# Trace of a matrix product: the order of the five-row and the twelve-row loads

## The chip, the cores and the metric

The kernel runs on one core of a Trainium2 chip. The time is device microseconds of one execution; three runs of the kernel before gave 709.28 us (median; 708.98 to 710.05).

## The reference

For eight pairs of 2176 x 2176 matrices in float32, the kernel returns the trace of each product:

```python
prod = np.matmul(a, b)                      # a, b: (8, 2176, 2176)
traces = np.diagonal(prod, axis1=1, axis2=2).sum(axis=-1)
```

The product itself is not needed: trace(A B) is the sum over all i, k of A[i, k] B[k, i], so the sum of the elementwise product of A transposed with B. Each element of a and b is read once, 303 MB in all.

## The kernel before, in words

A matrix of 2176 rows is 17 row tiles of 128 rows (`NT`). They are split into two groups of six and one of five (`SIX`, `FIVE`, `TWICE` = 12). In a group of m row tiles, partition p holds the m consecutive rows p*m to p*m + m - 1, so that each partition is filled by one long run. All loads of the loop are issued by GpSimd and cast float32 to bf16 on the way (`fetch`).

There are four large buffers in bf16. `a_six` and `b_six` hold the twelve rows of a and of b. `five` holds the five rows: first those of a, then those of b of the same batch. `at` holds the whole transposed a of one batch.

Per batch:

- TensorE transposes a in 26 tiles (`EACH`): 18 for the twelve rows, 8 for the five (`HEAD` is the count of the tiles of the group that comes first). A tile is six or five transposes of pairs of bf16 columns read as float32 (line 224), or up to fifteen of single columns (line 227). It goes into one of three PSUM slots (`slots`). TensorE waits for the load of a group on the semaphore `moved`, which SyncE counts up when a load of a has landed (lines 172 and 173), and for a free slot; it counts finished tiles in `made`.
- ScalarE evicts three of four tiles to `at` (line 269), VectorE every fourth (line 295). The first eviction of a batch waits until the products of the batch before are through, because these read `at`.
- When all 26 tiles are evicted, VectorE multiplies `at` with b and reduces (line 284): once for the twelve rows, once for the five, each as soon as its load has landed. `product` counts these, two a batch.

What sets the order of the work is written out by hand. GpSimd's queue issues, in each batch, a's twelve rows, a's five, b's twelve, b's five; each load waits on the semaphore that says that its buffer's old content is used up (`made` for a, `product` for b). Loads on one queue run one after the other. In batch 0, the first row of each partition comes by a load of SyncE in float32, lands in `b_six`, and is cast to its place by ScalarE and VectorE (lines 262 and 281).

In the last batch (`LAST`), b comes in nine pieces (`pieces`), so that little work is left behind the last bytes. `shares` says for each piece which columns VectorE multiplies; the rest goes to TensorE as 128 x 128 matmuls into `trace_ps` (line 253), whose diagonal VectorE takes at the end. The third number of a share is a count of filler matmuls, whose result is not used (line 255). A last row of small matmuls (line 333) sums over the partitions; VectorE copies the result (line 338) and SyncE stores it.

Of the kernel before, what the change touches and what calls it, by code (L numbers as in the profile page):

```python
# [21 lines left out]
def kernel(  # L22
# [6 lines left out]
    nc = tc.nc  # L29
    P = 128  # L30
    BATCH, N, N2 = a.shape
    assert N == N2 and N % P == 0
    NT = N // P
    SIX, FIVE = 6, 5
    TWICE = 2 * SIX
# [7 lines left out]
    HALF = 8 * P  # L43
# [6 lines left out]
    a_six = big.tile([P, TWICE, N], bf16, tag="a_six")  # L50
    b_six = big.tile([P, TWICE, N], bf16, tag="b_six")
    five = big.tile([P, FIVE, N], bf16, tag="five")
# [14 lines left out]
    def tiles_of(rows, start, m):  # L67

        words = rows.bitcast(f32)
        dst = at[:, :, start:start + P * m].rearrange("q v (p r) -> q v p r", r=m)  # L70
        pairs, singles = [], []
        for first, bm in groups:
            v = first // P
            if bm % 2 == 0:
                for t in range(bm // 2):
                    pairs.append((v + 2 * t, first // 2 + t, bm // 2))
            else:
                singles += [(v + r, first + r, bm) for r in range(bm)]
        for v, c0, step in pairs:
            yield (  # L80
                [(f32, r, words[:, r, c0:c0 + step * (P - 1) + 1:step]) for r in range(m)],
                dst[:, v:v + 2, :, :],
                lambda ps: ps[:, 0:m, :].bitcast(bf16).rearrange("q r (p s) -> q s p r", s=2),
            )
        each = 16 // m
        for at0 in range(0, len(singles), each):
            some = singles[at0:at0 + each]
            yield (
                [
                    (bf16, n * m + r, rows[:, r, c0:c0 + step * (P - 1) + 1:step])  # L90
                    for n, (_, c0, step) in enumerate(some) for r in range(m)
                ],
                dst[:, some[0][0]:some[0][0] + len(some), :, :],
                lambda ps, k=len(some): ps.bitcast(bf16).rearrange("q a b -> q (a b)")[
                    :, 0:k * m * P
                ].rearrange("q (n r p) -> q n p r", r=m, p=P),
            )

    six_tiles = [
        t for g in range(2)  # L100
        for t in tiles_of(a_six[:, g * SIX:(g + 1) * SIX, :], g * SIX * P, SIX)
    ]
    five_tiles = list(tiles_of(five, TWICE * P, FIVE))
    tiles = six_tiles + five_tiles
    EACH, HEAD = len(tiles), len(six_tiles)
    on_vector = [n for n in range(EACH) if n % 4 == 3]
    on_scalar = [n for n in range(EACH) if n % 4 != 3]

    def flat(t):
        return t.rearrange("p r k -> p (r k)")  # L110

    def six(src):
        return src[0:TWICE * P, :].rearrange("(g p r) k -> p g (r k)", g=2, r=SIX)

    def rows_of(src, start, m, r0, r1):
        return src[start:start + P * m, :].rearrange("(p r) k -> p (r k)", r=m)[:, r0 * N:r1 * N]

    by_twos = "p (g r) k -> p g (r k)"
# [7 lines left out]
    class Piece:  # L126
# [8 lines left out]
            self.src = src[:, r0 * N + lo:(r1 - 1) * N + hi]  # L135

    pieces = [
        Piece(0, 6), Piece(6, 10), Piece(10, 12), Piece(12, 14), Piece(14, 15), Piece(15, 16),
        Piece(16, 17, 6 * P, N), Piece(16, 17, 2 * P, 6 * P), Piece(16, 17, 0, 2 * P),
    ]  # L140


    shares = [
        (0, N, 0), (0, N, 0), (0, 0, 7), (0, 0, 6), (0, N, 0), (HALF, N, 2),
        (6 * P, 11 * P, 0), (0, 0, 0), (0, 0, 0),
    ]

    with tc.tile_critical(no_gpsimd_drain=True):  # L148
        def counted(name):
            return Counted(nc, name)  # L150

        first_row, first_five = counted("first_row"), counted("first_five")
        d_a6, d_a5, d_b6, d_b5 = (counted(f"load_{x}") for x in ("a6", "a5", "b6", "b5"))
        d_late = [counted(f"late{n}") for n in range(len(pieces))]
        zeros, ready, cast = counted("zeros"), counted("ready"), counted("cast")
        moved, made = nc.alloc_semaphore("moved"), nc.alloc_semaphore("made")
        free = [nc.alloc_semaphore(f"free{k}") for k in range(SLOTS)]
        scalar_done, vector_done = counted("scalar_done"), counted("vector_done")
        product, early, added = counted("product"), counted("early"), counted("added")
# [3 lines left out]

        sp = nc.sync
        words = flat(b_six[:, 0:2, :].bitcast(f32))
        first_row.by(sp.dma_start(out=words, in_=rows_of(a[0], 0, SIX, 0, 1)), 16)
        for n in range(BATCH):
            if n == 0:
                sp.wait_ge(cast.sem, 2)
                sp.wait_ge(first_five.sem, 16)  # L170
            for load in (d_a6, d_a5):
                sp.wait_ge(load.sem, 16 * (n + 1))
                sp.sem_inc(moved)


        gp = nc.gpsimd

        def fetch(count, dst, src):
            count.by(gp.dma_start(out=dst, in_=src), 16)  # L179

        for n in range(BATCH):
            if n == 0:
                fetch(first_five, flat(a_six[:, 1:SIX, :]), rows_of(a[0], 0, SIX, 1, SIX))
                fetch(d_a6, flat(a_six[:, SIX:, :]), rows_of(a[0], SIX * P, SIX, 0, SIX))
                gp.wait_ge(zeros.sem, 2)
                for t in (identity32, identity16):
                    ready.by(gp.affine_select(
                        out=t, in_=t, compare_op=mybir.AluOpType.not_equal, fill=1.0, base=0,
                        pattern=[[-1, P]], channel_multiplier=1,
                    ))  # L190
            else:
                gp.wait_ge(made, EACH * (n - 1) + HEAD)
                fetch(d_a6, a_six.rearrange(by_twos, g=2), six(a[n]))
                gp.wait_ge(product.sem, 2 * n)
            fetch(d_a5, flat(five), rows_of(a[n], TWICE * P, FIVE, 0, FIVE))
            if n == 0:
                gp.wait_ge(cast.sem, 2)
            else:
                gp.wait_ge(product.sem, 2 * n - 1)
            if n < LAST:  # L200
                fetch(d_b6, b_six.rearrange(by_twos, g=2), six(b[n]))
                gp.wait_ge(made, EACH * (n + 1))
                fetch(d_b5, flat(five), rows_of(b[n], TWICE * P, FIVE, 0, FIVE))
                continue
            for k, piece in enumerate(pieces):
                if piece.v0 == TWICE:
                    gp.wait_ge(made, EACH * (n + 1))
                fetch(d_late[k], piece.dst, piece.src)
        gp.drain()


# [35 lines left out]
        for w in work:  # L247
            k, x, y = w
# [10 lines left out]
        middle = N // 2  # L259
        act = nc.scalar  # L260
        act.wait_ge(first_row.sem, 16)
        cast.by(act.copy(out=a_six[:, 0, :middle], in_=words[:, :middle]))  # L262
        for n in range(BATCH):
            for t in on_scalar:
                _, dst, view = tiles[t]
# [10 lines left out]
        dve = nc.vector  # L276
# [1 line left out]
        for t in (identity32, identity16):  # L278
            zeros.by(dve.memset(t, 0.0))
        dve.wait_ge(first_row.sem, 16)  # L280
        cast.by(dve.tensor_copy(out=a_six[:, 0, middle:], in_=words[:, middle:]))  # L281

        def multiply_reduce(x, y, acc, out=None):
            return dve.tensor_tensor_reduce(  # L284
# [4 lines left out]
        for n in range(BATCH):  # L289
            for t in on_vector:  # L290
                _, dst, view = tiles[t]
                if t == on_vector[0] and n:
                    dve.wait_ge(product.sem, 2 * n)
                dve.wait_ge(made, EACH * n + t + 1)
                ins = dve.tensor_copy(out=dst, in_=view(slots[t % SLOTS]))  # L295
                if t != on_vector[-1]:
                    ins.then_inc(free[t % SLOTS], 1)
                else:
                    vector_done.by(ins)
            dve.wait_ge(vector_done.sem, n + 1).then_inc(free[on_vector[-1] % SLOTS], 1)  # L300
            dve.wait_ge(scalar_done.sem, n + 1).then_inc(free[on_scalar[-1] % SLOTS], 1)
            if n == LAST:
                continue
            for k, (load, t, v0) in enumerate(((d_b6, b_six, 0), (d_b5, five, TWICE))):
                dve.wait_ge(load.sem, 16 * (n + 1))
                product.by(multiply_reduce(
                    flat(at[:, v0:v0 + t.shape[1], :]), flat(t), sums[:, 2 * n + k:2 * n + k + 1],
                ))
        dve.wait_ge(early.sem, 1)
        dve.reduce_sum(  # L310
            out=result[:1, 0:LAST],
            in_=total[:, 0:2 * LAST].rearrange("o (b n) -> o b n", n=2),
# [3 lines left out]
        for k, (piece, (lo, hi, _)) in enumerate(zip(pieces, shares)):  # L316
            if hi > lo:
                dve.wait_ge(d_late[k].sem, 16)
                t, base = (b_six, 0) if piece.v0 < TWICE else (five, TWICE)
# [11 lines left out]
        for c in range(cols):  # L331
# [9 lines left out]
            out=out.rearrange("(a b) -> a b", a=1), in_=result[:1, :],  # L341
# [34 lines left out]
```

## Time and profile before

| | |
|---|---|
| median of the runs | 709.28 us |
| the profiled execution: span from its first to its last instruction (the page gives no other time of its own) | 706.8 us |
| share of the span in which engines are busy | PE 26%, DVE 54%, ACT 29%, POOL 4% |
| HBM read | 303.04 MB, 429 GB/s over the span |
| mean granted TensorE clock | 0.671 |

PE is TensorE's matmul, PEld its weight load, DVE VectorE, ACT ScalarE, POOL GpSimd, SP SyncE. A row of a time line is: start in us, length in us, engine, line, operation, out<-in, shapes, number of instructions merged into it, and in brackets the idle time just before it with what ended it. The length of a DMA instruction in such a row is the time that its issue took, not the transfer. A row of a group ends with: busy us, mean ns of one, and idle us before them. A row of a table of windows has the window, its length, the busy time of PE, PEld, DVE, ACT and POOL with their counts, the granted clock, the DMA share and the GB/s written.

### The profile page before, as it was taken

The page shows a single profiled execution, that of the slowest core. Times are in us where ns is not written, and L with a number is a line of the kernel's source. Part 1 is how long each engine was busy: PE and PEld are TensorE (multiplying, and loading weights), DVE is VectorE, ACT ScalarE, POOL GpSimd, SP SyncE. Part 2 cuts the span into 40 slices and gives each one's busy share as a digit, 9 for nine tenths or more (in the row PEclk, how much of TensorE's full clock was granted, in tenths as well). Part 3 has the DMA queues.
Part 4 walks back from the last instruction along what each step waited for, and adds up shares of the span by engine and source line. Part 5 has one row for each costly group of instructions (what it writes and reads, how often), then busy time and mean ns, then how long its engine had stood idle before and what let it go on. Part 6 is the DMA issues. An engine that isn't in the chain of part 4 may idle for free. (4 is left out here: it accounts for less than half of the span.)

```text
span 706.8 us, 3878 instructions
## 1 busy us (share of the span) xinstructions
PE 183.1 (26%) x1611; PEld 164.7 (23%) x1613; DVE 380.7 (54%) x94; ACT 203.8 (29%) x162; POOL 24.9 (4%) x46
## 2 busy tenths in 40 slices
PE   0083000830008200182002710027100370003706
PEld 0073000720007200172002710027100270003704
DVE  0031596315963169531794407944089440894487
ACT  1085000950009400094001930019200292002910
POOL 1000000000000000000000000000000000001010
PEclk9998555975559755597555965559655596555967
DMA  9999999999999999999999999999999999999997
GB/s 221 221 220 212 213 229 204 215 225 213 216 217 219 214 220 217 210 217 223 215 216 216 219 219 218 214 216 219 216 218 213 217 220 217 214 217 215 219 209 156
DMA packets 7702, 152.13 MB, mean 215 GB/s; under 512 B 658, under 2 KB 914, under 8 KB 1298
## 3 DMA queue, kind: packets, MB, share of 16 engines
q0 software_dynamic: 7552, 150.96, 99.7%
q1 hardware_dynamic: 146, 1.11, 0.5%
q8 instruction: 2, 0.03, 0.0%
q14 instruction: 2, 0.02, 0.0%
HBM read 303.04 MB, written 0.00 MB: 429 GB/s over the span
## 5 line engine op out<-in xcount | busy, mean ns | idle before, releaser
L269 ACT COPY at<-aT 128x1536 bf16<-128x1536 bf16 (+3 forms) x160 | 201.4, 1367 | 465.7 <-PE aT L224 465.2
L284 DVE CUSTOM_DVE_ANT_0 at<-at,b_six 128x26112 bf16<-128x26112 bf16 (+2 forms) x9 | 214.4, 23831 | 130.1 <-DMA b_six<-in_b_dram 130.0
L224 PE MATMUL aT<-identity,a_six 128*128 128x128 f32 x576 | 92.0, 324 | 482.5 <-PEq L221 482.5
L224 PEld LDWEIGHTS aT<-identity,a_six 128*128 128x128 f32 x576 | 85.7, 206 | 488.0 <-issue 487.9
L295 DVE COPY at<-aT 128x1536 bf16<-128x1536 bf16 (+1 forms) x48 | 80.1, 1669 | 183.3 <-PE aT L224 152.4
L284 DVE CUSTOM_DVE_ANT_0 at<-at,five 128x10880 bf16<-128x10880 bf16 (+3 forms) x10 | 85.0, 8501 | 1.0 <-DMA five<-in_b_dram 1.0
L227 PE MATMUL aT<-identity,a_six 128*128 128x128 bf16 x480 | 33.5, 219 | 11.6 <-PEq L221 11.4
L224 PE MATMUL aT<-identity,five 128*128 128x128 f32 x240 | 34.6, 289 | 4.4 <-PEq L221 4.4
L227 PEld LDWEIGHTS aT<-identity,a_six 128*128 128x128 bf16 x480 | 29.3, 118 | 15.6 <-issue 15.6
L224 PEld LDWEIGHTS aT<-identity,five 128*128 128x128 f32 x240 | 30.4, 198 | 7.4 <-issue 7.0
L179 POOL DMA_DIRECT2D five<-in_a_dram x8 | 4.4, 556 | 388.7 <-DVE sums L284 388.7
L179 POOL DMA_DIRECT2D five<-in_b_dram x13 | 7.1, 558 | 257.0 <-PE aT L227 257.0
L227 PE MATMUL aT<-identity,five 128*128 128x128 bf16 x200 | 13.9, 219 | 2.8 <-PEq L221 1.8
L227 PEld LDWEIGHTS aT<-identity,five 128*128 128x128 bf16 x200 | 11.9, 118 | 5.1 <-issue 5.1
L253 PE MATMUL trace_ps<-b_six,at 128*128 128x128 bf16 x34 | 3.8, 313 | 18.0 <-DMA b_six<-in_b_dram 18.0
L253 PEld LDWEIGHTS trace_ps<-b_six,at 128*128 128x128 bf16 x34 | 3.5, 149 | 18.1 <-issue 18.1
L179 POOL DMA_DIRECT2D b_six<-in_b_dram x10 | 6.6, 662 | 3.8 <-ACT a_six L262 3.8
L179 POOL DMA_DIRECT2D a_six<-in_a_dram x9 | 6.2, 688 | 1.0 <-SPq L148 1.0
L255 PE MATMUL aT<-at 128*128 128x512 bf16 x13 | 4.2, 462 | 0.3 <-issue 0.2
L253 PE MATMUL trace_ps<-five,at 128*128 128x128 bf16 x54 | 3.8, 220 | 1.6 <-DMA five<-in_b_dram 1.5
L253 PEld LDWEIGHTS trace_ps<-five,at 128*128 128x128 bf16 x54 | 3.1, 98 | 3.1 <-DMA five<-in_b_dram 2.7
L281 DVE CAST a_six<-b_six 128x1088 bf16<-128x1088 f32 x1 | 0.7, 726 | 4.8 <-DMA b_six<-in_a_dram 4.8
(19 smaller groups left out, 8.8 us busy)
## 6 DMA issues: line engine op xcount, KB each, us to landing
b_six<-in_b_dram POOLq DMA_DIRECT2D x7, 6528.0 KB, 47.6
a_six<-in_a_dram POOLq DMA_DIRECT2D x7, 6528.0 KB, 61.0
five<-in_a_dram POOLq DMA_DIRECT2D x8, 2720.0 KB, 17.4
five<-in_b_dram POOLq DMA_DIRECT2D x7, 2720.0 KB, 30.7
a_six<-in_a_dram POOLq DMA_DIRECT2D x1, 3264.0 KB, 32.2
b_six<-in_b_dram POOLq DMA_DIRECT2D x1, 3264.0 KB, 32.3
a_six<-in_a_dram POOLq DMA_DIRECT2D x1, 2720.0 KB, 17.5
b_six<-in_b_dram POOLq DMA_DIRECT2D x1, 2176.0 KB, 42.0
```

The source lines that it names most:

```text
L179: count.by(gp.dma_start(out=dst, in_=src), 16)
L224: last = pe.transpose(ps[:, place, :], src, identity32)
L227: last = pe.transpose(ps16[:, place * P:(place + 1) * P], src, identity16)
L253: ins = pe.matmul(trace_ps, x, y, start=w is real[0], stop=w is real[-1])
L255: pe.matmul(slots[0][:, 0:4, :], x, y, start=True, stop=True)
L269: ins = act.copy(out=dst, in_=view(slots[t % SLOTS]))
L281: cast.by(dve.tensor_copy(out=a_six[:, 0, middle:], in_=words[:, middle:]))
L284: return dve.tensor_tensor_reduce(out=x if out is None else out, in0=x, in1=y, scale=1.0, scalar=0.0, op0=MUL, op1=ADD, accum_out=acc,)
L295: ins = dve.tensor_copy(out=dst, in_=view(slots[t % SLOTS]))
```

## The change

The order of the groups is turned round: in each matrix the five-row group is loaded, transposed and multiplied ahead of the twelve rows. GpSimd now issues a's five rows, a's twelve, b's five, b's twelve. With it go these:

- The tiles of the five rows come first (`tiles`, `HEAD` = 8), and VectorE multiplies the five rows first.
- a's five rows wait for the five-row product of the batch before (`five` is free), a's twelve for all tiles of the batch before, b's five for the eight tiles of a's five, b's twelve for the twelve-row product of the batch before.
- In batch 0, SyncE's first row belongs to the five-row group. The twelve rows of a come in one load; before, they came as two loads of six (the first without its first row).
- In the last batch the pieces of b are: the five rows; the first six; two rows; three single rows; the last of the twelve rows in three parts. VectorE has the five, the six and parts of the last two rows; TensorE has the rest, with 21 filler matmuls (before: 15).
- GpSimd makes twenty increments of a semaphore that nothing reads, behind its last load and ahead of its drain.

```diff
-    tiles = six_tiles + five_tiles
-    EACH, HEAD = len(tiles), len(six_tiles)
+    tiles = five_tiles + six_tiles
+    EACH, HEAD = len(tiles), len(five_tiles)
...
     pieces = [
-        Piece(0, 6), Piece(6, 10), Piece(10, 12), Piece(12, 14), Piece(14, 15), Piece(15, 16),
-        Piece(16, 17, 6 * P, N), Piece(16, 17, 2 * P, 6 * P), Piece(16, 17, 0, 2 * P),
+        Piece(TWICE, NT), Piece(0, 6), Piece(6, 8), Piece(8, 9), Piece(9, 10), Piece(10, 11),
+        Piece(11, 12, 6 * P, N), Piece(11, 12, 2 * P, 6 * P), Piece(11, 12, 0, 2 * P),
     ]
...
     shares = [
-        (0, N, 0), (0, N, 0), (0, 0, 7), (0, 0, 6), (0, N, 0), (HALF, N, 2),
+        (0, N, 0), (0, N, 0), (0, 0, 7), (0, 0, 6), (0, 0, 6), (HALF, N, 2),
         (6 * P, 11 * P, 0), (0, 0, 0), (0, 0, 0),
     ]
...
-        first_row.by(sp.dma_start(out=words, in_=rows_of(a[0], 0, SIX, 0, 1)), 16)
+        first_row.by(sp.dma_start(out=words, in_=rows_of(a[0], TWICE * P, FIVE, 0, 1)), 16)
...
-                sp.wait_ge(first_five.sem, 16)
-            for load in (d_a6, d_a5):
+            for load in (d_a5, d_a6):
...
             if n == 0:
-                fetch(first_five, flat(a_six[:, 1:SIX, :]), rows_of(a[0], 0, SIX, 1, SIX))
-                fetch(d_a6, flat(a_six[:, SIX:, :]), rows_of(a[0], SIX * P, SIX, 0, SIX))
+                fetch(d_a5, flat(five[:, 1:, :]), rows_of(a[0], TWICE * P, FIVE, 1, FIVE))
+                fetch(d_a6, a_six.rearrange(by_twos, g=2), six(a[0]))
...
             else:
-                gp.wait_ge(made, EACH * (n - 1) + HEAD)
+                gp.wait_ge(product.sem, 2 * n - 1)
+                fetch(d_a5, flat(five), rows_of(a[n], TWICE * P, FIVE, 0, FIVE))
+                gp.wait_ge(made, EACH * n)
                 fetch(d_a6, a_six.rearrange(by_twos, g=2), six(a[n]))
-                gp.wait_ge(product.sem, 2 * n)
-            fetch(d_a5, flat(five), rows_of(a[n], TWICE * P, FIVE, 0, FIVE))
-            if n == 0:
-                gp.wait_ge(cast.sem, 2)
-            else:
-                gp.wait_ge(product.sem, 2 * n - 1)
+            gp.wait_ge(made, EACH * n + HEAD)
             if n < LAST:
+                fetch(d_b5, flat(five), rows_of(b[n], TWICE * P, FIVE, 0, FIVE))
+                if n == 0:
+                    gp.wait_ge(cast.sem, 2)
+                else:
+                    gp.wait_ge(product.sem, 2 * n)
                 fetch(d_b6, b_six.rearrange(by_twos, g=2), six(b[n]))
-                gp.wait_ge(made, EACH * (n + 1))
-                fetch(d_b5, flat(five), rows_of(b[n], TWICE * P, FIVE, 0, FIVE))
                 continue
             for k, piece in enumerate(pieces):
-                if piece.v0 == TWICE:
-                    gp.wait_ge(made, EACH * (n + 1))
+                if k == 1:
+                    gp.wait_ge(product.sem, 2 * n)
                 fetch(d_late[k], piece.dst, piece.src)
+        for _ in range(20):
+            gp.sem_inc(unread)
         gp.drain()
...
-        cast.by(act.copy(out=a_six[:, 0, :middle], in_=words[:, :middle]))
+        cast.by(act.copy(out=five[:, 0, :middle], in_=words[:, :middle]))
...
-        cast.by(dve.tensor_copy(out=a_six[:, 0, middle:], in_=words[:, middle:]))
+        cast.by(dve.tensor_copy(out=five[:, 0, middle:], in_=words[:, middle:]))
...
-            for k, (load, t, v0) in enumerate(((d_b6, b_six, 0), (d_b5, five, TWICE))):
+            for k, (load, t, v0) in enumerate(((d_b5, five, TWICE), (d_b6, b_six, 0))):
```

More of the change, by code (lines that the diff above doesn't have):

```diff
@@ L150, in counted @@
             return Counted(nc, name)
-        first_row, first_five = counted("first_row"), counted("first_five")
+        first_row, unread = counted("first_row"), nc.alloc_semaphore("unread")
         d_a6, d_a5, d_b6, d_b5 = (counted(f"load_{x}") for x in ("a6", "a5", "b6", "b5"))
```

## The prediction

> **What bounds the kernel now.** I read the page's slices first (is there one resource that never rests?), then the chain that ended last, then the time lines of GpSimd, ScalarE, VectorE and TensorE in the last batch. The slices and the note under the queues:
>
> ```profile
> DMA  9999999999999999999999999999999999999997
> HBM read 303.04 MB, written 0.00 MB: 429 GB/s over the span
> ```
>
> The transfers are busy from the first slice to the last but one, and no engine is. The chain (start, length, what):
>
> ```profile
> 674.65 28.38 DMA five<-in_b_dram
> ...
> 703.07 0.61 PE trace_ps L253 x6
> ...
> 703.71 0.29 DVE diagonal L284
> ...
> 704.29 0.15 DVE result L338
> ```
>
> So before the change the end is: last bytes of b at 703.03, six small matmuls, the diagonal on VectorE at 703.71, the result. Whatever the change does, it must show either as a hole in the stream of transfers or as an engine that reaches 703.71 late.
>
> How fast the stream is, I take from TensorE's first transpose of a batch, which waits for the twelve rows of a (batches 1 and 7):
>
> ```profile
> 123.10 4.34 PE L224 MATMUL aT<-identity,a_six 128*128 128x128 f32 x24 [62.38 <-PEq L221]
> ...
> 646.83 6.80 PE L224 MATMUL aT<-identity,a_six 128*128 128x128 f32 x36 [62.13 <-PEq L221]
> ```
>
> Six batches lie between: 523.73 / 6 = 87.29 us a batch of 34 row tiles, 2.567 us a row tile (1.09 MB in bf16). Twelve rows take 30.8 us, five 12.8 us.
>
> **Can the stream run dry in the new order?** The loads wait for buffers, so what counts is how long before its predecessor has landed a load is issued. GpSimd's issues in batch 7 and the six-row product of the batch before:
>
> ```profile
> 602.85 27.36 DVE L284 CUSTOM_DVE_ANT_0 at<-at,b_six 128x26112 bf16<-128x26112 bf16 x1 [18.72 <-DMA b_six<-in_b_dram]
> 630.14 0.08 DVE L284 DVE_READ_ACCUMULATOR2_ANT sums<- 128x1 f32 x1
> 630.14 11.48 DVE L284 CUSTOM_DVE_ANT_0 at<-at,five 128x10880 bf16<-128x10880 bf16 x1
> 641.55 0.08 DVE L284 DVE_READ_ACCUMULATOR2_ANT sums<- 128x1 f32 x1
> ...
> 641.93 0.56 POOL L179 DMA_DIRECT2D five<-in_a_dram  x1 [55.66 <-DVE sums L284]
> 642.48 1.60 POOL L179 DMA_DIRECT2D b_six<-in_b_dram  x3
> 672.57 3.18 POOL L179 DMA_DIRECT2D five<-in_b_dram  x6 [28.49 <-PE aT L227]
> ```
>
> Before, the tightest issue is a's five rows: at 641.93, 4.9 us ahead of 646.83, when the twelve rows were in. In the new order there are two issues to look at.
>
> b's five rows wait until the eight tiles of a's five rows are transposed, and those evictions wait for the twelve-row product of the batch before. That product starts five rows later than now: 602.85 + 5 x 2.567 = 615.69, ends 27.29 later at 642.98. ScalarE then has six of the eight tiles:
>
> ```profile
> L269 ACT COPY at<-aT 128x1280 bf16<-128x1280 bf16 x40 | 47.4, 1273 | 0.0
> L269 ACT COPY at<-aT 128x1920 bf16<-128x1920 bf16 x8 | 14.1, 1759 | 0.5
> ```
>
> 5 x 1.27 + 1.76 = 8.1 us, so at the latest at 651.1 all eight are transposed. The twelve rows of a are in at 646.83 + 12.84 = 659.67: a lead of 8.6 us. a's five rows of the next batch wait for b's five-row product: twelve rows of a in, 20.0 us of evictions (below), 0.41, 11.41 of product = 31.8 us; b's twelve rows are in 17 x 2.567 = 43.6 us after a's: a lead of 11.8. Both are longer than the 4.9 us that suffices now, so I cost the stream at nothing in all seven batches and at the start, where 17 rows are queued at once. The POOL waits that change places (the product ahead of a's loads, the count of tiles ahead of b's) hold up only those loads, and these leads are their price. At the start one load fewer is issued (a's twelve rows whole): I take 0, between -0.7, its issue, and +0.5, the small hole quoted under the rivals.
>
> Against this stands a rule: the Trainium skill, page "DMA: Bandwidth & Descriptors", section "Anatomy of one DMA", gives each GpSimd load a fixed 2.0 us beside bytes / 436 GB/s. Taken as time of the stream, an estimate from that page would make the missing load worth 2 us and the result about 710.8. But four loads of 2 x 18.9 MB read would then need 87 + 8 = 95 us a batch by it, and the trace has 87.29: the fixed part lies under the neighbours here.
>
> **The last batch, where the cost is.** The work after the last load is what moves. VectorE may multiply only when all 26 tiles of the last a are evicted. Now the twelve rows come first and ScalarE starts on them while the five are under way:
>
> ```profile
> 648.44 4.12 ACT L269 COPY at<-aT 128x1536 bf16<-128x1536 bf16 x3 [61.67 <-PE aT L224]
> 652.77 4.83 ACT L269 COPY at<-aT 128x1536 bf16<-128x1536 bf16 x4 [0.21 <-PE aT L224]
> 658.02 16.32 ACT L269 COPY at<-aT 128x1536 bf16<-128x1536 bf16 x13 [0.42 <-PE aT L224]
> ...
> 666.70 3.57 ACT L269 COPY at<-aT 128x1280 bf16<-128x1280 bf16 x3
> ```
>
> The last row (a view of a narrow window) is the first copy of a five-row tile: so the eighteen twelve-row tiles are evicted some 0.1 after 666.70, 20.0 us after the first transpose at 646.83. After the change these same eighteen tiles are all left to do when the last of a lands: eighteen tiles in the same pattern (positions 3, 7, 11 and 15 on VectorE), while the eight others are done by about 652. Evicted: 659.67 + 20.0 = 679.67, instead of 658.02 + 16.32 = 674.34. That is 5.3 us later, and the product follows there:
>
> ```profile
> 674.48 0.16 DVE L310 TENSOR_REDUCE result<-total 1x7 f32<-1x14 f32 x1 [2.78 <-ACT at L269]
> 674.75 13.76 DVE L284 CUSTOM_DVE_ANT_0 at<-at,b_six 128x13056 bf16<-128x13056 bf16 x1
> 688.44 0.08 DVE L284 DVE_READ_ACCUMULATOR2_ANT late<- 128x1 f32 x1
> ...
> 698.05 2.42 DVE L284 CUSTOM_DVE_ANT_0 at<-at,five 128x2176 bf16<-128x2176 bf16 x1 [0.39 <-DMA five<-in_b_dram]
> ...
> 700.66 1.36 DVE L284 CUSTOM_DVE_ANT_0 at<-at,five 128x1152 bf16<-128x1152 bf16 x1 [0.18 <-DMA five<-in_b_dram]
> 701.95 0.08 DVE L284 DVE_READ_ACCUMULATOR2_ANT late<- 128x1 f32 x1
> 702.42 0.82 DVE L284 CUSTOM_DVE_ANT_0 at<-at,five 128x640 bf16<-128x640 bf16 x1 [0.39 <-DMA five<-in_b_dram]
> 703.17 0.08 DVE L284 DVE_READ_ACCUMULATOR2_ANT late<- 128x1 f32 x1
> ```
>
> The first product started 0.41 after the last eviction, so now at 680.08. VectorE's share keeps its size (five, six, then 9 and 5 blocks of 128; before six, four, one, 9 and 5): 11.41 (630.14 to 641.55) + 13.69 (674.75 to 688.44) + 1.29 + 0.75 = 27.14 us from start to start, without any wait, since b's five rows are in at 672.5, the next six at 687.9, and the small pieces before VectorE gets to them. It is through at 707.22, and the diagonal starts there rather than at 703.71: **+3.5 us**. Before, the same work had slack: its waits for pieces (0.18 and twice 0.39) show VectorE ahead of the transfers.
>
> TensorE's share is also later. It starts on rows 6 and 7 one row later than on rows 10 and 11 before, and has six filler matmuls more:
>
> ```profile
> 690.36 3.79 PE L253 MATMUL trace_ps<-b_six,at 128*128 128x128 bf16 x34 [17.97 <-DMA b_six<-in_b_dram]
> 694.37 2.36 PE L255 MATMUL aT<-at 128*128 128x512 bf16 x6 [0.22 <-issue]
> 696.56 2.06 PE L253 MATMUL trace_ps<-five,at 128*128 128x128 bf16 x34
> 698.46 1.46 PE L255 MATMUL aT<-at 128*128 128x512 bf16 x6
> 700.68 0.62 PE L253 MATMUL trace_ps<-five,at 128*128 128x128 bf16 x8 [0.77 <-DMA five<-in_b_dram]
> ```
>
> 692.93 + 6.20 (34 and 7 fillers) + 2 x (0.95 + 1.46) + 0.68 + 0.8 (2 fillers) + 0.8 (12 matmuls) = 706.2. It no longer waits for pieces and would put the end 2.5 us later by itself, but it lies beside VectorE's 707.2.
>
> The twenty increments stand behind GpSimd's last load, which is issued by about 656 (nine pieces of 0.56 after 651.1). Even at a load's 0.56 each they would be over at 668, under the products; nothing waits for the count, so neither gain nor cost: 0. Without that cover, at the very end, they would be up to 11 us. The cast of the first row goes to another buffer at the same length: 0. What follows the diagonal is as before, one small matmul fewer.
>
> Sum: span 706.8 + 3.5 = 710.3. The median of the runs, 709.28, is 2.5 above the profiled span (launch and store around it), and I add the same: **712.8 us**, 0.5% slower. Against 0.2% of noise, 1.4 us, that can be told.
>
> **Terms that are not exact.** The landing at 659.67 could be 659.4, counted back 17 rows from 703.03: -0.3. Evictions of a whole batch took 28.0 us from the first transpose in batch 0 (34.78 to 62.79, the two rows below) and 27.5 in batch 7 (646.83 to 674.34): +0.5.
>
> ```profile
> 34.78 7.10 PE L224 MATMUL aT<-identity,a_six 128*128 128x128 f32 x36 [34.78 <-PEq L221]
> ...
> 46.47 16.32 ACT L269 COPY at<-aT 128x1536 bf16<-128x1536 bf16 x13 [0.42 <-PE aT L224]
> ```
> The landing of seventeen rows rests on the batches' rate; a hole as below in the first or a later batch adds up to 0.5 each, and three or four of them make +2. A VectorE path shorter than I think stops at TensorE's 706.2, +2.5. So 711.2 to 715.0.
>
> **The rivals.**
>
> TensorE ends last: if evictions end 1 us or more sooner than 679.67, the diagonal waits for its matmuls at 706.2, and the time is 711.8. Against it is only the sum above; 13 in 100.
>
> The stream runs dry: the 8.6 us lead of b's five rows is not enough, each batch has a hole. With 1 us in each of seven the last rows land 7 us later and the time is about 719.8. Against it: 4.9 us suffices now. 6 in 100.
>
> On the other side: the present 4.9 us is too short, and each batch now loses time which the longer leads give back. Three microseconds around that landing, in batch 1 and in batch 7, and the long stretch between:
>
> ```profile
> 121.00:124.00 3.00, 0.90 (x5) 0.93 (x6) 0.00 (x0) 0.00 (x0) 0.00 (x0) 0.50 0.82 167
> 644.60:647.60 3.00, 0.77 (x4) 0.80 (x5) 0.00 (x0) 0.00 (x0) 0.00 (x0) 0.50 0.99 210
> ...
> 124.00:646.00 522.00, 126.66 (x1119) 115.27 (x1118) 292.75 (x60) 150.99 (x120) 16.07 (x26) 0.64 1.01 217
> ```
>
> In batch 1 the DMA share (the last but one number) is 0.82, 0.5 us lost; seven such would be 3.8 us, and the time 709.0, no change. From 0.3 us in each batch on (2.1 in all) the result is within the noise. Against it: 0.99 in batch 7 and 1.01 over all. 5 in 100 for no change, 2 for an outright gain.
>
> **How the numbers follow.** VectorE late, 712.8: 74 in 100. With TensorE's case, 87 end slower; with the dry stream 93. Unchanged 5 and faster 2 are the regained holes. The range 711.2 to 715.0 covers the first two cases.
>
> **What would show it.** Right: the DMA rows unbroken; a's twelve rows of the last batch landing near 659.7; the last eviction near 679.7; VectorE without a wait for DMA from there to the diagonal near 707.2; the chain that ended last made of VectorE and before it ScalarE instead of DMA. Wrong: the diagonal's idle time put down to TensorE, or VectorE waiting for pieces of b (the shift was smaller), or a long wait of SyncE for a's rows in each batch (the stream ran dry).

## The result, and the profile after

| | before | after |
|---|---|---|
| median of the runs (8 each) | 709.24 us | 711.72 us (711.13 to 712.06) |
| ratio, 95% interval | | 1.0031 (1.0021 to 1.0041) |
| span of the profiled execution | 706.8 us | 709.8 us (that execution: 711.61 us) |

The change costs 2.5 us, 0.3%. The page of the changed kernel, its DMA slices and the shares of the chain that ended last:

```profile
DMA  9999999999999999999999999999999999999995
...
DVE 4%; ACT 1%; PE 0%; issue 0%; DVEq 0%
```

The transfers fill every slice but the last, as before, but the chain no longer ends in a transfer. It is now made of VectorE and, before it, ScalarE. The same chain in order of time (start, length, what):

```profile
670.50 8.87 ACT at L270 x7
...
679.50 0.16 DVE result L311
679.66 11.41 DVE at L285
...
691.08 13.67 DVE at L285
...
704.76 1.27 DVE at L285
...
706.03 0.74 DVE at L285
...
707.27 0.15 DVE result L339
```

These are ScalarE's last evictions, then the five rows, the first six rows and the two parts of rows, all on VectorE without a pause. Nothing in it waits for b. The time line of the last batch shows what each of these follows:

```profile
649.22 0.56 POOL L178 DMA_DIRECT2D five<-in_b_dram  x1 [44.26 <-PE aT L228]
649.78 4.25 POOL L178 DMA_DIRECT2D b_six<-in_b_dram  x8
659.30 6.74 PE L225 MATMUL aT<-identity,a_six 128*128 128x128 f32 x36 [10.38 <-PEq L222]
660.86 4.12 ACT L270 COPY at<-aT 128x1536 bf16<-128x1536 bf16 x3 [10.28 <-PE aT L225]
...
670.50 8.86 ACT L270 COPY at<-aT 128x1536 bf16<-128x1536 bf16 x7 [0.40 <-PE aT L225]
...
679.59 11.48 DVE L285 CUSTOM_DVE_ANT_0 at<-at,five 128x10880 bf16<-128x10880 bf16 x1
...
704.13 0.83 PE L254 MATMUL trace_ps<-b_six,at 128*128 128x128 bf16 x12
...
706.70 0.28 DVE L285 CUSTOM_DVE_ANT_0 diagonal<-identity,trace_ps 128x128 bf16<-128x128 f32 x1
```

a's twelve rows are in at 659.30, 12.5 us later than before (646.83). ScalarE evicts the eighteen tiles until 670.50 + 8.86 = 679.36. VectorE starts at 679.59 (674.75 before), and the diagonal comes at 706.70 (703.71 before), 1.7 us after TensorE's last matmul of b. So the profiled spans differ by 3.0 us and the medians by 2.5. The difference has two parts. The execution that was profiled before stood 0.5 us under the usual span of its kernel (706.8 against a median of 707.3 to 707.4 in the runs beside the variants), and this led to a second finding (below). And the time outside the span, launch and store, is not the same in both: 1.9 to 2.2 us in those runs of the kernel before, 1.7 to 1.8 in the eight of the changed kernel.

### The profile page after: what moved, and what is told of

It reads as the page before. It is cut to its first block, busy times and chain, and to the rows that moved or that the text cites. A ratio compares the mean times of both kernels' runs of the same rounds, so it can differ in the third digit from the quotient of the medians.

```text
span 709.8 us, 3904 instructions
## 1 busy us (share of the span) xinstructions
PE 207.4 (29%) x1617; PEld 187.4 (26%) x1617; DVE 380.9 (54%) x92; ACT 205.1 (29%) x162; POOL 24.8 (3%) x45
## 3 DMA queue, kind: packets, MB, share of 16 engines
q1 hardware_dynamic: 146, 1.11, 0.4%
HBM read 303.04 MB, written 0.00 MB: 427 GB/s over the span
## 5 line engine op out<-in xcount | busy, mean ns | idle before, releaser
L285 DVE CUSTOM_DVE_ANT_0 at<-at,b_six 128x26112 bf16<-128x26112 bf16 (+3 forms) x10 | 207.3, 20743 | 82.1 <-DMA b_six<-in_b_dram 82.1
L225 PE MATMUL aT<-identity,five 128*128 128x128 f32 x240 | 55.0, 419 | 367.9 <-PEq L222 367.9
L225 PEld LDWEIGHTS aT<-identity,five 128*128 128x128 f32 x240 | 47.3, 221 | 373.8 <-issue 373.8
L285 DVE CUSTOM_DVE_ANT_0 at<-at,five 128x10880 bf16<-128x10880 bf16 x8 | 91.9, 11491 | 14.3 <-ACT at L270 14.3
L228 PE MATMUL aT<-identity,five 128*128 128x128 bf16 x200 | 16.9, 258 | 0.0
L228 PEld LDWEIGHTS aT<-identity,five 128*128 128x128 bf16 x200 | 16.6, 132 | 0.4
L178 POOL DMA_DIRECT2D five<-in_b_dram x8 | 4.5, 563 | 334.5 <-PE aT L228 334.5
L254 PE MATMUL trace_ps<-b_six,at 128*128 128x128 bf16 x88 | 7.5, 254 | 14.4 <-DMA b_six<-in_b_dram 14.4
L254 PEld LDWEIGHTS trace_ps<-b_six,at 128*128 128x128 bf16 x88 | 6.9, 116 | 15.5 <-issue 14.7
L178 POOL DMA_DIRECT2D b_six<-in_b_dram x15 | 9.2, 636 | 0.0
```

The costliest lines, as they stand in the source:

```text
L225: last = pe.transpose(ps[:, place, :], src, identity32)
L228: last = pe.transpose(ps16[:, place * P:(place + 1) * P], src, identity16)
L254: ins = pe.matmul(trace_ps, x, y, start=w is real[0], stop=w is real[-1])
L285: return dve.tensor_tensor_reduce(out=x if out is None else out, in0=x, in1=y, scale=1.0, scalar=0.0, op0=MUL, op1=ADD, accum_out=acc,)
```

## The experiments

Each variant was run beside the kernel before on the same chip (whose medians there were 709.30 to 709.37 us). What is given is the median of the runs, then the ratio to the kernel before with its 95% interval.

**The increments.** Edit:

```diff
-        for _ in range(20):
-            gp.sem_inc(unread)
```

> The changed kernel without the twenty increments. Theory (VectorE's late start in the last batch is the whole cost): 711.7 us as with them, since GpSimd's last load is issued at 649.8 + 4.25 = 654.0, more than 50 us before the end. Rival (the increments delay the drain or the end): the time falls by what they cost, up to the whole 2.5 us, to 709.2.

Measured: 711.73 us, 1.0031 (1.0019 to 1.0044), the same as with them, so they cost nothing that can be measured. But the time outside the span is 1.95 to 2.18 us, and with them it was 1.72 to 1.81; the total is the same because the spans of these runs are a little shorter. So the increments may even save some 0.3 us outside the span. This is not shown: in the variants below that relieve both engines, which have the increments too, it is up to 2.7 us.

**Is it TensorE's longer list?** Edit, in the shares:

```diff
-        (0, N, 0), (0, N, 0), (0, 0, 7), (0, 0, 6), (0, 0, 6), (HALF, N, 2),
+        (0, N, 0), (0, N, 0), (0, 0, 7), (0, 0, 0), (0, 0, 6), (HALF, N, 2),
```

> The changed kernel without the six filler matmuls behind row 8, so with 15 as before the change. Theory: VectorE ends last, TensorE only beside it (its last matmul of b ended at 704.96, VectorE's share at 706.70), so 711.7 us, unchanged, with TensorE through about 2 us earlier. Rival (TensorE's longer list sets the end): about 2 us less, 709.7 us.

Measured: 711.43 us, 1.0029 (1.0018 to 1.0040). TensorE's last matmuls of b and the diagonal:

```profile
702.90 0.83 PE L254 MATMUL trace_ps<-b_six,at 128*128 128x128 bf16 x12
...
706.78 0.28 DVE L285 CUSTOM_DVE_ANT_0 diagonal<-identity,trace_ps 128x128 bf16<-128x128 f32 x1
```

TensorE was through with b at 703.73 instead of 704.96, the diagonal still came at 706.78, and the time stayed. TensorE is not the end.

**Less work for VectorE.** Edit: two of b's five rows become a piece of their own that TensorE multiplies.

```diff
-        Piece(TWICE, NT), Piece(0, 6), Piece(6, 8), ...
+        Piece(TWICE, 15), Piece(15, NT), Piece(0, 6), Piece(6, 8), ...
...
-        (0, N, 0), (0, N, 0), (0, 0, 7), (0, 0, 6), (0, 0, 6), (HALF, N, 2),
+        (0, N, 0), (0, 0, 0), (0, N, 0), (0, 0, 7), (0, 0, 6), (0, 0, 6), (HALF, N, 2),
```

> The changed kernel with two of b's five rows given to TensorE as a piece of their own, which it can do at 680, where it has nothing else. VectorE has 4.6 us less to do. Theory: VectorE is through at about 703.0, when the last bytes are in; then TensorE is last, with its last matmul of b at about 705.0, so the diagonal starts there and the time falls by about 1.7 us to 710.0. Rival (the stream of transfers or the launch is what became longer, not VectorE): no change, 711.7 us.

Measured: 709.49 us, 1.0001 (0.9992 to 1.0010). The end of its time line on VectorE:

```profile
687.32 13.76 DVE L285 CUSTOM_DVE_ANT_0 at<-at,b_six 128x13056 bf16<-128x13056 bf16 x1 [1.05 <-DMA b_six<-in_b_dram]
...
703.02 0.08 DVE L285 DVE_READ_ACCUMULATOR2_ANT late<- 128x1 f32 x1
704.78 0.29 DVE L285 CUSTOM_DVE_ANT_0 diagonal<-identity,trace_ps 128x128 bf16<-128x128 f32 x1 [1.68 <-PE trace_ps L254]
```

VectorE is ahead again: it waits for b at 687 and is through at 703.02, as expected. The diagonal then waits 1.68 us for TensorE, which is the next in line. The time fell by 2.2 us where 1.7 was expected, and the kernel is level with the one before.

**Both engines relieved.** Edit: the two rows on TensorE, and its filler matmuls 7, 0, 6, 2; in a second variant 7, 0, 3, 1.

```diff
-        (0, N, 0), (0, N, 0), (0, 0, 7), (0, 0, 6), (0, 0, 6), (HALF, N, 2),
+        (0, N, 0), (0, 0, 0), (0, N, 0), (0, 0, 7), (0, 0, 0), (0, 0, 3), (HALF, N, 1),
```

> Two of b's five rows given to TensorE and six filler matmuls fewer. Theory: with both engines relieved the end follows the last bytes again, which in the changed kernel landed no later than before: 709.2 us, the whole loss back (708.7 to 709.6). Rival (the new order itself costs time in the stream or at the start): it stays above 710.5 us.

> Two of b's five rows on TensorE, and ten filler matmuls fewer than the changed kernel has (seven, three and one are left). Theory: in the variant with six fewer, TensorE ran from 692.6 to 703.5 without waiting for the last pieces, some 0.5 us behind the last bytes; with four fewer still it waits for them, so about 708.2 us, as long as its clock stays up. Rival (the transfers already set the end there): 708.7 us, unchanged. If TensorE's clock falls for want of fillers: 709 us or more.

Measured: 708.69 us, 0.9991 (0.9982 to 1.0000), and with the second (the lean one) 708.40 us, 0.9990 (0.9981 to 0.9999). The end of the chain of the second:

```profile
654.61 48.16 DMA b_six<-in_b_dram
...
703.47 0.29 DVE diagonal L285
```

The end hangs on the transfers again, and the time is not that of the kernel before but 0.9 us under it (0.7 in the first variant). So the change also gains something that the late VectorE had hidden. The rival in which the new order costs time elsewhere is out. The lean variant came out between its theory (708.2) and its rival (708.7).

**Only the last batch as before.** Edit: batches 0 to 6 and the start in the new order; in batch 7 a's twelve rows ahead of its five, and the old pieces and shares (tiles, waits and TensorE's loop by batch).

```diff
-    tiles = five_tiles + six_tiles
+    orders = [five_tiles + six_tiles] * LAST + [six_tiles + five_tiles]
...
-            for load in (d_a5, d_a6):
+            for load in ((d_a5, d_a6) if n < LAST else (d_a6, d_a5)):
...
+                if n == LAST:
+                    gp.wait_ge(made, EACH * n)
+                    fetch(d_a6, a_six.rearrange(by_twos, g=2), six(a[n]))
                 gp.wait_ge(product.sem, 2 * n - 1)
                 fetch(d_a5, flat(five), rows_of(a[n], TWICE * P, FIVE, 0, FIVE))
```

> The new order in batches 0 to 6 and at the start; the last batch alone as before (a's twelve rows, a's five, and the old pieces and shares). Theory: the cost lies in the last batch alone, so 709.2 us or a little less (708.6 to 709.4). Rival (the new order costs something in every batch): at least 711.0 us.

Measured: 708.35 us, 0.9988 (0.9979 to 0.9997), with the lean variant the fastest, in a band of 708.24 to 708.50 over 11 runs, where the kernel before ran from 708.38 to 709.86. This splits the change: the last batch costs 711.72 - 708.35 = 3.4 us, and the rest of it gains 709.34 - 708.35 = 1.0 us. Of this 1.0, 0.7 lie in the span (medians 707.3 and 706.6) and the rest outside it, where this variant has 1.8 us and the kernel before 2.0.

**Start or lead?** The gain could come from the start (one load fewer) or from the lead, the time from the issue of a load to the landing of the one ahead of it. Three runs were made to tell these apart. The first has batch 0 alone in the new order:

```diff
-    tiles = six_tiles + five_tiles
+    orders = [five_tiles + six_tiles] + [six_tiles + five_tiles] * LAST
...
-                fetch(first_five, flat(a_six[:, 1:SIX, :]), rows_of(a[0], 0, SIX, 1, SIX))
-                fetch(d_a6, flat(a_six[:, SIX:, :]), rows_of(a[0], SIX * P, SIX, 0, SIX))
+                fetch(d_a5, flat(five[:, 1:, :]), rows_of(a[0], TWICE * P, FIVE, 1, FIVE))
+                fetch(d_a6, a_six.rearrange(by_twos, g=2), six(a[0]))
```

> Batch 0 in the new order (with the new start and a's twelve rows as one load), batches 1 to 7 in the old one with the old pieces. The variant with only the last batch old ran at 708.35 us in a narrow band, 1.0 us under the kernel before. Theory A (that gain lies in the lead: 4.9 us for a's five rows in the old order, 8 us and more in the new one): 709.2 us, like the kernel before, with its spread of about 1.4 us, since batches 1 to 7 have the short lead again. Theory B (the gain lies in the start: one load fewer): 708.4 us, with a narrow band.

Measured: 709.53 us, 1.0005 (0.9996 to 1.0014), from 708.60 to 710.66. In the median the new start alone gains nothing, and the wide band is back. (Its trace shows some gain all the same; see the third run.)

The second takes lead away from the variant with only the last batch old:

```diff
                 gp.wait_ge(made, EACH * n + HEAD)
+                if n:
+                    for _ in range(6):
+                        gp.wait_ge(held.sem, held.by(gp.memset(scratch, 0.0)))
```

> The variant with only the last batch old, with six fills of an unused 128 x 1024 tile on GpSimd, one behind the other, ahead of each issue of b's five rows in batches 1 to 6. That takes some 5 us from their lead of 8 to 10 us. Theory A (a lead of about 5 us is too short in some batches): about 709.2 us, and a wider band than 708.24 to 708.50. Theory B (the lead plays no part down to 5 us): 708.4 us, in the same narrow band. If the fills take longer than 8 us, the stream runs dry and the time rises by about 3 us a batch.

Measured: 716.99 us, 1.0109 (1.0094 to 1.0124), from 715.14 to 718.15. One of the six places, on GpSimd and then on TensorE:

```profile
303.81 6.00 POOL L206 MEMSET scratch<- 128x1024 f32 x6 [47.21 <-PE aT L241]
310.11 0.56 POOL L181 DMA_DIRECT2D five<-in_b_dram  x1 [0.30 <-POOL scratch L206]
...
313.13 5.40 PE L238 MATMUL aT<-identity,a_six 128*128 128x128 f32 x30 [9.38 <-PEq L235]
```

The fills with their waits took 6.3 us, more than meant: the load is issued at 310.11 and TensorE has a's twelve rows at 313.13, a lead of 3.0. So this is not the lead of 5 us that the expectation spoke of, and a lead of that length in the new order stays untested. But it shows that a short lead costs time while the load is still issued ahead of the landing: 8.6 us in the median, 1.4 us for each of the six batches. The price does not follow from the lead alone. In the profiled execution (715.14 us) TensorE starts on the twelve rows of batches 1 to 6 at distances of 87.87, 89.67, 87.92, 88.10 and 88.61 us instead of 87.29: leads of 3.0, 2.6, 3.0, 2.7 and 3.9 us cost 0.6, 2.4, 0.6, 0.8 and 1.3, and the sixth, of 3.8, cost 0.1. That is 5.8 of the 6.8 us by which this execution is longer; the rest comes in the last batch and is not explained.

The third profiles the kernel before once more:

> The kernel before, unchanged, profiled once more: its profiled execution had a span of 706.8 us, and the changed kernel's executions are all 1.8 us longer than their spans, so it stood for about 708.6 us, 0.7 under the median of its runs. Theory A: an execution near the median (709.3 us, span 707.5) shows pauses of some tenths of a us in the stream where a's five rows follow the twelve. Theory B: no pauses there, but a later start.

Measured: 709.44 us at a span of 707.4, so 2.0 us outside the span. (By this figure, and not by the changed kernel's 1.8, the first profile of 706.8 stood for about 708.8 us.) TensorE's first transposes of batches 1 to 4 in it:

```profile
123.25 4.19 PE L224 MATMUL aT<-identity,a_six 128*128 128x128 f32 x24 [62.53 <-PEq L221]
...
210.80 5.47 PE L224 MATMUL aT<-identity,a_six 128*128 128x128 f32 x30 [62.42 <-PEq L221]
...
298.32 6.80 PE L224 MATMUL aT<-identity,a_six 128*128 128x128 f32 x36 [62.41 <-PEq L221]
...
385.60 5.47 PE L224 MATMUL aT<-identity,a_six 128*128 128x128 f32 x30 [61.77 <-PEq L221]
```

The batches take 87.55, 87.52 and 87.28 us, where those of the first profile took 87.24 to 87.34: two of the three are a quarter of a microsecond too long. Of its 0.6 us more in span these two make 0.5. So the execution on which the prediction rests was one of the luckier ones of its kernel, and losses of a quarter of a microsecond, in some batches, are what this execution, near the median, has and that one hardly had. Where they stand is told by the landings. A row of the DMA issues ends with the time from issue to landing; a's five rows of batch 1 in the first profile, then those of batches 1 and 2 in this one:

```profile
five<-in_a_dram POOLq DMA_DIRECT2D x1, 2720.0 KB, 17.4
...
five<-in_a_dram POOLq DMA_DIRECT2D x1, 2720.0 KB, 17.7
...
five<-in_a_dram POOLq DMA_DIRECT2D x1, 2720.0 KB, 17.5
```

In batches 3 and 4 it is 17.4 again. So the quarter of batch 1 stands where a's five rows follow the twelve, and a part of that of batch 2. That the lead of 4.9 us is what causes it is the reading that the three runs agree with; no run has the old order with a long lead, and the profiled execution of the first run has leads of 4.8 us and no such batch.

These losses are not the whole gain. In the variant with only the last batch old, TensorE starts on the twelve rows of batches 1 and 7 here:

```profile
135.56 6.74 PE L233 MATMUL aT<-identity,a_six 128*128 128x128 f32 x36 [10.48 <-PEq L230]
...
646.39 7.09 PE L233 MATMUL aT<-identity,a_six 128*128 128x128 f32 x36 [55.59 <-PEq L230]
```

In batch 1 the new order has landed five row tiles more, 12.84 us, so the old order's 123.25 corresponds to 136.09: 0.5 us are gained before batch 1 is under way (0.4 against the first profile's 123.10). At batch 7 as many rows have landed in both, and it is 647.48 against 646.39: 1.1 us. So in these two traces about half of the gain is there by batch 1, and half comes in the batches after it. The first run agrees: its trace has batch 1 at 122.85, 0.25 to 0.4 us sooner than the two profiles of the kernel before. The scatter of its runs hides this in the median, and neither of its theories holds alone.

**No lead at all.** Edit: `gp.wait_ge(made, EACH * n + HEAD + 1)` in the changed kernel, so that b's five rows wait for the first tile of a's twelve.

> The changed kernel with b's five rows held back until the first tile of a's twelve rows is transposed, that is until after these rows have landed: the lead of 8 to 10 us becomes about -2 us in all eight batches. Theory: each batch gets a hole of 3.5 to 4.5 us (0.5 to the transpose, 1.3 for the tile, 0.6 to issue, and the load's own start), eight of them, so 736 to 744 us, and SyncE's waits grow by that. If a load's start costs little (1 us): about 720 us. If the leads were already the limit in the changed kernel, it would have shown holes there, which its trace does not.

Measured, in one execution: 752.93 us, 41.2 us more than the changed kernel, 5.2 us a batch and more than expected. Windows around the first hole (the last two numbers are the DMA share and GB/s):

```profile
44.00:45.00 1.00, 0.00 (x0) 0.00 (x0) 0.00 (x0) 0.00 (x0) 0.00 (x0) 0.50 1.94 418
45.00:46.00 1.00, 0.00 (x0) 0.00 (x0) 0.00 (x0) 0.00 (x0) 0.00 (x0) 0.50 0.00 0
...
49.00:50.00 1.00, 1.00 (x6) 1.00 (x5) 0.00 (x0) 1.00 (x1) 0.76 (x2) 0.50 0.00 0
50.00:51.00 1.00, 1.00 (x7) 1.00 (x6) 0.00 (x0) 1.00 (x2) 0.52 (x1) 0.50 1.66 239
...
44.80:44.90 0.10, 0.00 (x0) 0.00 (x0) 0.00 (x0) 0.00 (x0) 0.00 (x0) 0.50 2.43 522
44.90:46.30 1.40, 0.00 (x0) 0.00 (x0) 0.00 (x0) 0.00 (x0) 0.00 (x0) 0.50 0.00 0
...
46.90:50.50 3.60, 3.08 (x15) 3.11 (x16) 0.00 (x0) 1.52 (x2) 1.26 (x2) 0.50 0.00 0
50.50:50.60 0.10, 0.10 (x2) 0.10 (x1) 0.00 (x0) 0.10 (x1) 0.01 (x1) 0.50 9.40 1306
```

and the work around it:

```profile
47.42 5.65 PE L225 MATMUL aT<-identity,a_six 128*128 128x128 f32 x30 [23.00 <-PEq L222]
...
49.24 0.56 POOL L178 DMA_DIRECT2D five<-in_b_dram  x1 [45.78 <-PE aT L225]
```

The share of 1.94 in a window of 1 us shows how to read these rows: a packet is counted whole in the window in which it starts. One packet on each of the 16 engines started between 44 and 45, and each took 1.94 us. So a window of 0.00 behind them is not yet a standstill (the changed kernel, whose stream goes on, has 1.94 and 0.00 in the same two windows). The last of them started before 44.90 and ended at about 46.8; the next packets start after 50.50. The DMA engines thus stand still for 3.7 us. TensorE moves at 47.42, 0.6 us after the last packet ended; the load is issued 1.8 us later, at 49.24, and its first packets come 1.3 us after that. The other 1.5 of the 5.2 us are not accounted for.

**Other shares for the evictions.** Edit: VectorE evicts `n % 3 == 2` rather than `n % 4 == 3`.

> The changed kernel with VectorE evicting every third tile instead of every fourth, in all batches. ScalarE then has 12 of the last eighteen tiles (12 x 1.33 = 16.0 us and 1.6 ahead) instead of 14. Theory: the last eviction ends some 2.5 us sooner, at about 677, VectorE's share with it at about 704.3, and TensorE's (705.0) becomes last: about 710.0 us. Rival (the lateness does not come from the evictions of the eighteen tiles): 711.7 us.

Measured: 710.68 us, 1.0021 (1.0012 to 1.0031): the right way, but 1.0 us of the 1.7 that were expected, and VectorE is still last. The eighteen tiles there:

```profile
660.90 1.76 DVE L296 COPY at<-aT 128x1536 bf16<-128x1536 bf16 x1 [11.79 <-PE aT L225]
...
662.18 2.78 ACT L270 COPY at<-aT 128x1536 bf16<-128x1536 bf16 x2 [10.83 <-PE aT L225]
...
671.01 7.77 ACT L270 COPY at<-aT 128x1536 bf16<-128x1536 bf16 x6 [0.73 <-PE aT L225]
```

The first tile now falls to VectorE, ScalarE begins 1.3 us later (662.18 against 660.86) and waits more for TensorE (0.73 against 0.40 us in the last of the rows), and ends at 678.78 instead of 679.36, 0.6 us sooner where 2.5 were expected. So taking tiles from ScalarE helps little here; the added waits for TensorE's tiles are the likely reason.

## Why the prediction was right, and where its size was off

The forecast was 712.8 us (711.2 to 715.0); it is 711.72.

- The stream does not run dry in the new order: right. The lead of b's five rows in the last batch is 659.30 - 649.22 = 10.1 us (8.6 was worked out as the least).
- The landing of a's twelve rows in the last batch: 659.30 against 659.67. The 0.37 us are there from the start, which was taken at 0 between -0.7 and +0.5: in batch 1 TensorE begins at 135.57 against 123.10 + 12.84 = 135.94, and the six batches from there take 523.73 us in both profiles.
- Eviction of the eighteen tiles in 20.0 us from the first transpose: 679.36 - 659.30 = 20.1, as read off the old trace at 666.70.
- VectorE's share of 27.14 us without a wait: 706.70 - 679.59 = 27.11. Its begin was 0.23 behind the last eviction, not 0.41. The diagonal came at 706.70 against 707.22. That this path is the end is shown by the variant with two rows fewer on VectorE, and its price by the one with the old last batch: 3.4 us, where 3.5 was worked out.
- TensorE beside it, at 706.2: it was through at 704.96. It began 0.4 us earlier than worked out (692.50 against 692.93), and the lengths of merged rows were added whole, although the next group starts before such a row ends. As a rival it was rightly not the end, but it was the next in line, as the diagonal's 1.68 us of waiting shows.
- The increments at nothing: right in the total; a saving of some 0.3 us outside the span is not excluded.
- The sum: here the size was off, by 1.1 us. The span of 710.3 was 709.8 in the profile, mostly by the earlier landing. The larger part is the term of 2.5 us, "launch and store around it". The kernel before's own runs are about 2.0 us longer than their spans; the other 0.5 was what the profiled execution lay under the median. The changed kernel has 1.8 in that place, so the term was 0.7 too large. With it goes "I cost the stream at nothing in all seven batches": against the median as a base, the new order does not only keep the stream whole, it saves time that the median run loses at the start and between the loads. By the variants the account is +3.4 for the late VectorE and -1.0 for the rest: +2.4, measured +2.5.
- That gain was the rival on the other side, priced as all or nothing, at 3.8 us or none, from one window. The window's 0.82 was no loss: packets are counted whole where they start, so the share of a window of 3 us depends on where it is cut. The batch around it took 210.39 - 123.10 = 87.29 us, like the others. So the rival named a gain that is real, but its price rested on a misread window. The gain is 1.0 us, a part of it at the start, and it stands beside the late VectorE instead of against it.
- "4.9 us suffices now" was read from an execution that had nearly none of these losses; its batches of 87.29 us looked like the limit of the stream, and no profile has them clearly shorter, but the median run's are not all of that length.
- A row tile is 1.11 MB in float32 and 0.56 MB in bf16 (303.04 MB are 272 of them), not 1.09 MB in bf16; no sum uses the figure.

## What to carry to other kernels

Where transfers bound a kernel, the order of the loads matters at the end: what has to be done between the landing of the last operand that needs much work and the first use of it is the tail, so load that operand early, and count for each engine what is left after it. A load that waits for a buffer should be issued well ahead of the landing before it; here the short lead showed as scatter of the runs, and in only one of two profiles. When a sum is made against one profiled execution, compare its span with the spans of the other runs first: the half microsecond between them was time that the change could win back, and not launch. When two profiles are compared, ask whether a gain is there from the first batch or grows from batch to batch.

## What the hardware showed beyond this

How a lead is paid, from issue to the moment when TensorE starts on the load ahead: with 8.7 to 10.1 us (the changed kernel) the twelve rows of batches 1 to 7 follow each other at 87.24 to 87.33 us, so nothing is lost; with 4.9, two batches of one profile are a quarter of a microsecond longer and none of another; with 2.6 to 3.9, a batch loses between 0.1 and 2.4 us, 1.4 in the median run; with -1.8, 5.2 us. Between the last packet's end and TensorE's start lie 0.6 us, and between a load's issue and its first packets 1.3. By these two alone a lead of 2 us would do, so why 3 and more still lose time stays open.

The Trainium skill, page "DMA: Bandwidth & Descriptors", section "Anatomy of one DMA", has about 2 us of fixed time a load, most of it at the end of the transfer. Here the two parts make 1.9 us together, but most of it stands ahead of the first packet, and the 0.6 at the end still hold SyncE's hop to TensorE.
